# Moved weight loads, a third sample-state buffer, and two chunks of gate rows loaded first in the last stage of a hybrid decoder step

## The chip, the cores and the metric

The kernel runs on one core of one Trainium2 chip. The metric is the device time of one execution in microseconds. The core has four compute engines with a queue each, worked off strictly in order: PE (TensorE, matrix products and transposes), DVE (VectorE), ACT (ScalarE), POOL (GpSimd). SP (SyncE) issues DMAs here, and POOL issues some as well. An instruction that waits for a semaphore holds up everything behind it on its queue.

## The reference, cut to what matters

One step of a one-layer decoder: a joint input projection, then dilated window attention (8 heads of 64) beside an mLSTM (4 heads of 128, chunks of 128), each gated, then one output projection. It does so for a prompt of 2048 tokens and for 8 sample sequences of 4 tokens.

```python
u = rmsnorm(x, norm_g) @ w_in                      # q,k,v,z of attention | q,k,v,o,z,i,f of the mLSTM
# attention, for (window, dilation) in (128,1), (512,4), (2048,16): blocks of 128 queries by 256 keys
s = einsum(qs, kk) * HEAD_DIM_ATT ** -0.5; m = max(s); p = exp(s - m); den = sum(p); acc = einsum(p, vv)
y_a = combine(the three parts) * silu(za)
# mLSTM, chunk by chunk with the state C, n, m
dmat = exp(where(causal, b[t] - b[s] + i[s] - m_t, -inf))
num = inter * (qc @ C) + ((qc @ kc.T) * dmat) @ vc
C = decay * C + (w * kc).T @ vc
y_b = headnorm(sigmoid(ob) * num / den) * silu(zb)
y = rmsnorm(x + concat(y_a, y_b) @ w_out)
# outputs also: the new key/value windows (for the samples: the old cache shifted by 4 rows), and C, n, m
```

## The kernel before, in words

The kernel is written with a tile framework. A scheduler in it fixes at build time the order of the instructions on each engine; memory reuse becomes semaphore waits. `behind_all` and `issue_after` act on that order only. There are three stages.

The first (to about 560 us) makes the projections that attention needs, stores q, k, v to scratch in DRAM, and does the sample tokens' attention.

The second (about 560 to 877 us) is the prompt's attention: four pairs of heads, `pr` 0 to 3, two heads `h` each, 19 batches of at most 512 scores per head. `pair_loads` (L696) brings a pair's `qn` (1 MB) and `kn` (1.5 MB), single buffers. `stacks` (L708) transposes them on PE for one head: 16 blocks of `qn`, 32 of `kn`. A batch is then: scores on PE (L1046, L1047, `ps_s`), mask and minimum on DVE (L1055), shift on POOL (L1057) or ACT, exp on ACT, transposes on PE (L1068, `ps_t`), two halves by ACT and DVE (L1071, L1072), value products on PE (L1084 to L1086, `ps_o`). The values of a pair come in 1 + 4 + 16 loads, v2, v1 and v0 (L978, L981, L984). Into this stage the scheduler weaves the sample tokens' mLSTM, class `SampleMLSTM`: `prepare`, then for each of 8 sequences `state`, which loads a state matrix (L919, 256 KB), multiplies it, stores `dm_num` (L943), adds to it and stores it (L922). Into this stage it also weaves an early part of the last stage's projections (`early`, from `early_x` and the weight blocks `wb`, 2 MB each, loaded at L1117 and L1118 after the first head). `bulk` (L293) starts copies of 1 MB from DRAM to DRAM on POOL's queue, 64 in all, for the samples' new windows; three batches of each head start one (L1063 to L1065).

The last stage (about 877 to 1517 us) goes over 16 chunks of 128 tokens. For each it loads `z` (L1271), the attention parts `A` (L1273, 792 KB), the gate rows `Mb` and, but for chunk 0, `qi` (L1279, L1282; 256 KB each, a DRAM row spread over all partitions), and the residual `xn` (L1286). The mLSTM part adds the causal mask `big` to `Mb` on POOL (L1385), starts three bulk copies there, takes exp on ACT (L1389), multiplies with the scores into `W` on DVE (L1394), and PE makes `ps_num` from `W` (L1406). `merge` (L1424 on) joins the three attention parts. Woven between are the next chunks' projections: `ps_v`, `ps_og`, and `ps_qk` with a convolution on ACT (L1201, L1205), DVE (L1211) and POOL.

"Join" below is the passage from the second stage to the last. The opening of the last stage stands at L1499 to L1509 and the loop at L1518; `A` of chunk 0 needs the three stores of the last pair's attention parts (L1128 to L1130), which go through POOL's queue.

Of the kernel before, what the change touches and what calls it, by code (L numbers as in the profile page):

```python
# [16 lines left out]
ALU = mybir.AluOpType  # L17
# [4 lines left out]
P = 128  # L22
# [815 lines left out]
class SampleMLSTM:  # L838


    def __init__(self, G, I, O, T, pool, pp):
        self.G, self.I, self.O, self.pool, self.pp = G, I, O, pool, pp
        at = 0

        def cut(n, rows=P, back=None):
            nonlocal at
            if back is not None:
                return T[:rows, back:back + n]
            at += n
            return T[:rows, at - n:at]  # L850

        four = lambda x: x.rearrange("p (c b j) -> p c b j", c=8, b=NB)
        heads = lambda x: x.rearrange("p (h e) -> p h e", h=HB)
        self.pre = four(cut(8 * NB * 7))
        self.d, self.th, self.tmp = (four(cut(8 * NS)) for _ in range(3))
        self.cv = four(cut(8 * NB * 3))
        self.kw, self.kz = cut(512, NS, 0), cut(512, NS, 512)
        self.num = heads(cut(HB * 129, NTOK, 1024))
        at = 1024 + HB * 129
        self.qk = cut(8 * NS).rearrange("p (c r) -> p c r", c=8)  # L860
        self.u = cut(1024, NS, at)
        self.C = [heads(cut(HB * 129)) for _ in range(2)]
        self.Dm, self.W = heads(cut(HB * NS, NS)), heads(cut(HB * NS, NS))
        self.qi = heads(cut(HB * NS))
        self.sn = [cut(NS).rearrange("p (b h) -> p b h", h=HB) for _ in range(2)]
        self.bm = cut(NS + NB, NS)
        self.v = heads(cut(HB * 129, NS))

    def ps(self, name):
        return self.pp.tile([P, 512], F32, tag="d", name=name)  # L870
# [13 lines left out]
    def prepare(self):  # L884
# [27 lines left out]
        for h in range(HB):  # L912
            hs = slice(h * P, (h + 1) * P)
            nc.scalar.activation(self.kw[:, hs], pk[:NS, hs], AF.Copy, scale=G.scols[:, 1, h:h + 1])
        self.load(0)

    def load(self, b):
        nc = self.G.nc
        nc.sync.dma_start(out=self.C[b % 2][:, :, 0:128], in_=self.I["state_C"][b].rearrange("h d e -> d h e"))  # L919

    def store(self, b):
        self.G.nc.sync.dma_start(out=self.O["s_C"][b].rearrange("h d e -> d h e"), in_=self.C[b % 2][:, :, 0:128])  # L922

    def state(self, b):
        G, nc, v = self.G, self.G.nc, self.v
        if b:
            self.store(b - 1)
        if b + 1 < NB:
            self.load(b + 1)
        Cb = self.C[b % 2]  # L930
        nc.gpsimd.tensor_copy(Cb[:, :, 128], self.sn[0][:, b])
        rows = slice(b * NTOK, (b + 1) * NTOK)
        nc.gpsimd.tensor_scalar(self.kz, self.kw, self.bm[:, NS + b:NS + b + 1], 0.0, ALU.mult, ALU.add)
        num = self.num
        pn = self.ps("ps_dn")[:, 0:129]
        group = lambda h: pn[h * NS:h * NS + NTOK]
        for h in range(HB):
            nc.tensor.matmul(group(h), lhsT=self.W[:, h, rows], rhs=v[:, h], start=True, stop=False)
        for h in range(HB):
            nc.tensor.matmul(group(h), lhsT=self.qi[:, h, rows], rhs=Cb[:, h], start=False, stop=True)  # L940
        for h in range(HB):
            nc.scalar.activation(num[:, h], group(h), AF.Copy)
        nc.sync.dma_start(out=G.dm_num[rows], in_=num)  # L943
        for a in range(2):
            pc = self.ps("ps_dC")[:, 0:2 * 129].rearrange("p (h e) -> p h e", h=2)
            for j in range(2):
                h = 2 * a + j
                nc.tensor.matmul(pc[:, j], lhsT=self.kz[:, h * P:(h + 1) * P], rhs=v[:, h], start=True, stop=True)
                nc.vector.scalar_tensor_tensor(Cb[:, h], Cb[:, h], G.sdec[:, h * NB + b:h * NB + b + 1], pc[:, j], ALU.mult, ALU.add)
        nc.gpsimd.tensor_copy(self.sn[1][:, b], Cb[:, :, 128])  # L950
# [6 lines left out]
def phase_b(G, I, O, dT):  # L957

    nc, tc = G.nc, G.tc
    with ExitStack() as st:  # L960
# [74 lines left out]
        def head(L, h):  # L1035
# [4 lines left out]
            for nb, batch in enumerate(batches(units(st))):  # L1040
# [18 lines left out]
                        nc.scalar.activation(pr[:, x:x + n], sc[:, x:x + n], AF.Exp, scale=-1.0, bias=nm)  # L1059
                if by_pool:  # L1060
                    nc.scalar.activation(pr[:, :w], sc[:, :w], AF.Exp)
                if nb in (3, 9, 15):
                    beat = pool.tile([P, 1], F32, tag="beat", name="beat")  # L1063
                    bulk(G, 1, nc.gpsimd.tensor_copy(beat, nm))
                with tc.high_priority(offset=60):  # L1065
# [29 lines left out]
        def early():  # L1095
# [4 lines left out]
            for i in range(NO):  # L1100
                G.first.og.append((yield from G.mix.gate_steps(G.early_x, slice(i * P, (i + 1) * P), bank)))

        early = early()
        for pr in range(4):
            L = loads(pr)
            for h in range(2):
                if pr == h == 0:
                    SM.loads()
                n = 2 * pr + h
                if 1 <= n <= 4:  # L1110
                    SM.state(2 * n - 2)
                head(L, h)
                if pr == h == 0:
                    with behind_all(G, last_on(G, ENG.PE, ENG.Activation, ENG.DVE, ENG.Pool)):
                        SM.prepare()
                    for j in range(3):
                        nc.sync.dma_start(out=G.wb[j], in_=G.w_scr[j])  # L1117
                    nc.sync.dma_start(out=G.early_x.rearrange("p a k t -> p (a k t)"), in_=G.x_scr[0])  # L1118
                if 1 <= n <= 4:
                    SM.state(2 * n - 1)  # L1120
                if n == 4:
# [121 lines left out]
def phase_c(G, I, O):  # L1243

    nc, tc = G.nc, G.tc
    with ExitStack() as st:
# [17 lines left out]
            nc.sync.dma_start(out=x16.rearrange("p a k t -> p (a k t)"), in_=G.x_scr[g])  # L1264
            return x16

        def loads(c):
            rows = slice(c * P, (c + 1) * P)
            T = Ctx()
            T.z = pool.tile([P, 2, 512], F32, tag="z", name="z", bufs=2)  # L1270
            nc.sync.dma_start(out=T.z.rearrange("p a c -> p (a c)"), in_=G.z_scr[rows, :])  # L1271
            T.A = pool.tile([P, 3, HA, ROW], F32, tag="wf", name="A", bufs=2)
            nc.sync.dma_start(out=T.A.rearrange("p a (r h) e -> p (a r) (h e)", r=4), in_=G.att_scr.rearrange("a r t e -> t (a r) e")[rows])  # L1273
            return T

        def gate_rows(c, T):
            gr = G.g_scr.rearrange("a (h c) t -> a c h t", h=HB)
# [101 lines left out]
        def mlstm(c, T, qk, tok, v, og, y):  # L1379
            Mb = T.Mb  # L1380
            if c:
                qi = T.qi
                for h in range(HB):
                    nc.gpsimd.tensor_tensor(qi[:, h], qi[:, h], qk[h][:, tok], ALU.mult)  # L1384
            bulk(G, 3, nc.gpsimd.tensor_tensor(Mb, Mb, big.unsqueeze(1).broadcast_to([P, HB, P]), ALU.add))  # L1385
            ps = pp.tile([P, 512], F32, tag="st", name="ps_st", bufs=3)
            pk = pp.tile([P, 512], F32, tag="st", name="ps_kt", bufs=3)
            for h in range(HB):
# [111 lines left out]
        xg = [G.early_x, x_load(1)]  # L1500
        big = one.tile([P, P], F32, tag="big", name="big")
        nc.sync.dma_start(out=big, in_=I["c_causal"])
        L = loads(0)
        gate_rows(0, L)
        for j in range(2):
            nc.sync.dma_start(out=wo[j], in_=G.w_scr[4 + j])
        residual(0, L)
        fg = one.tile([P, D], F32, tag="fg", name="fg")
        nc.sync.dma_start(out=fg, in_=I["final_norm_g"].partition_broadcast(P))  # L1509
        prev = None  # L1510
# [7 lines left out]
        for c in range(NT - 1):  # L1518
# [13 lines left out]
            if c == 3:  # L1532
                run(sample)
            if c + 1 < NT:
                Ln = loads(c + 1)
            if prev is not None:
                next(prev)
                if c < NT - 2:
# [11 lines left out]
                sample = sample_out(ys)  # L1550
                next(sample)
            L = Ln
            gate_rows(c + 1, L)
        gate_rows(NT - 1, Ln)
        spare = G.early_x.rearrange("p a k t -> p (a k t)").bitcast(F32)
        yl = gated(NT - 1, Ln, qk, slice(P, 2 * P), vs[NT - 1], ogs[NT - 1], spare[:, :D])
# [183 lines left out]
```

## Time and profile before

| | us |
|---|---|
| three runs | 1514.84, 1516.72, 1519.55 (median 1516.72) |
| profiled execution, its own time | 1518.98 |
| its span (first to last instruction) | 1517.1 |
| PE busy | 1367.1 (90% of the span) |
| DVE busy | 982.2 (65%) |
| ACT busy | 739.1 (49%) |
| POOL busy | 468.3 (31%) |
| mean busy share of the 16 DMA engines, second stage | 0.5 to 0.9 by slices |

The span leaves out 1.88 us of the profiled execution (1518.98 - 1517.1). PE is busy nearly all of the time, so time can only go where PE stands idle or runs at the lower clock, or by taking work off it. A row of the trace's timeline gives the start, the duration, the engine, line, operation and tiles, and in brackets the idle time before it with what ended it. For an SP row the duration includes the time for which the issue was held up on its queue.

### The profile page before, as it was taken

Reading aid. Unit: us, or ns where it says so; the run is one execution under the profiler, and the core shown is the slowest. Engines: PE = TensorE matmul, PEld = TensorE weight load, DVE = VectorE, ACT = ScalarE, POOL = GpSimd, SP = SyncE. Lnnn points to the kernel's source line nnn. Section 1 sums busy time; section 2 is a strip of 40 time slices with the busy share of each in tenths; the row PEclk is TensorE's granted clock in tenths of the full one; section 3 lists DMA queues with packets and bytes.
Section 4 is the critical chain, followed back from the end, with each engine's and each line's share of the span. In section 5 each row is a group of like instructions: output and inputs, shape, how many; then the busy total and the mean of one; then the engine's idle time right before and its main releaser. Section 6 shows DMA issues by size and latency. Waiting matters only on the chain.

```text
span 1517.1 us, 29006 instructions
## 1 busy us (share of the span) xinstructions
PE 1367.1 (90%) x10679; PEld 851.1 (56%) x10679; DVE 982.2 (65%) x3054; ACT 739.1 (49%) x1701; POOL 468.3 (31%) x797
## 2 busy tenths in 40 slices
PE   4889998989999999579999986789899999999996
PEld 2345444444433348568789854455566666666653
DVE  5663775777643459478888805667766666666665
ACT  5265434454334339578888813344444444444432
POOL 1362334453310016344469922211211111111110
PEclk9999999999999999799999997989999999999999
DMA  8353588768769938884967765752656556643212
GB/s 296 111 181 135 177 284 297 275 218 309 269 216 381 331 128 284 306 264 156 278 216 234 280 218 173 206 174 75 213 161 190 161 188 160 187 161 106 78 48 77
DMA packets 153404, 310.96 MB, mean 205 GB/s; under 512 B 13533, under 2 KB 102782, under 8 KB 142686
## 3 DMA queue, kind: packets, MB, share of 16 engines
q1 hardware_dynamic: 149166, 230.10, 47.9%
q0 software_dynamic: 3952, 78.75, 14.3%
q8 instruction: 84, 1.38, 0.4%
q14 instruction: 58, 0.48, 0.1%
q10 hardware_dynamic: 144, 0.26, 0.0%
HBM read 231.80 MB, written 144.38 MB: 248 GB/s over the span
## 4 chain that ended last, share of the span: by engine, by line
PE 29%; DMA 21%; DVE 14%; issue 6%; ACT 6%; POOL 5%; SPq 2%; POOLq 0%; ACTq 0%; DVEq 0%
DMA Mb<-g_scr 5%; DMA qi<-g_scr 4%; PE ps_t L1068 3%; DVE cd L1211 3%; DMA qn<-q_scr 3%; POOL d_kv L396 2%; PE ps_out L184 2%; PE ps_out L182 2%; PE ps_out L183 2%; DMA v<-v_scr 2%; PE ps_proj L182 2%; PE ps_proj L183 2%; PE ps_proj L184 2%; DMA d_qb<-ds_scr 2%; PE ps_dv L445 2%
## 5 line engine op out<-in xcount | busy, mean ns | idle before, releaser
L182 PE MATMUL ps_proj<-wa,x 128*128 128x512 f16 x640 | 245.7, 386 | 17.9 <-DVE t L541 10.8
L183 PE MATMUL ps_proj<-wa,x 128*128 128x512 f16 x640 | 246.5, 386 | 2.3 <-POOL wa L128 2.0
L184 PE MATMUL ps_proj<-wa,x 128*128 128x512 f16 x640 | 246.5, 385 | 1.0 <-ACT x L243 1.0
L1055 DVE CUSTOM_DVE_ANT_0 sc<-ps_s,mask,ncqk 128x256 f32<-128x256 f32 (+1 forms) x384 | 143.7, 421 | 18.3 <-PE ps_s L1047 15.8
L1057 POOL TENSOR_SCALAR sc<-sc,o 128x256 f32<-128x256 f32 (+1 forms) x272 | 113.9, 430 | 95.7 <-DVE o L1055 90.2
L182 PEld LDWEIGHTS <-x 128*128 128x128 f16 x768 | 73.7, 99 | 100.8 <-issue 16.8
L1072 DVE SCALAR_TENSOR_TENSOR tl<-ps_t,th 128x512 f16<-128x512 f32 (+1 forms) x152 | 103.1, 680 | 38.3 <-ACT th L1071 37.5
L1211 DVE SCALAR_TENSOR_TENSOR cd<-pre,cw,cd 128x256 f32<-128x256 f32 x168 | 88.2, 531 | 53.7 <-ACT cd L1205 52.0
L184 PEld LDWEIGHTS <-x 128*128 128x128 f16 x768 | 73.4, 99 | 85.5 <-issue 12.3
L183 PEld LDWEIGHTS <-x 128*128 128x128 f16 x768 | 73.4, 99 | 77.9 <-issue 9.7
L396 POOL TENSOR_TENSOR d_kv<-d_kv,d_qb 128x512 f32<-128x512 f32 x64 | 85.9, 1376 | 90.7 <-DMA d_qb<-ds_scr 81.2
L1071 ACT ACTIVATE th<-ps_t 128x512 f16<-128x512 f32 (+1 forms) x152 | 90.5, 595 | 41.5 <-PE ps_t L1068 38.9
L184 PE MATMUL ps_out<-wo,yt 128*128 128x512 f16 x256 | 95.6, 382 | 7.8 <-DVE yt L1308 7.0
L1068 PE MATMUL ps_t<-c_id,pr 128*128 128x128 f32 x600 | 98.9, 285 | 2.9 <-DVE tl L1072 2.5
L182 PE MATMUL ps_out<-wo,yt 128*128 128x512 f16 x256 | 98.3, 384 | 3.3 <-ACT pre L1201 2.2
L183 PE MATMUL ps_out<-wo,yt 128*128 128x512 f16 x256 | 98.0, 383 | 0.0
L1385 POOL TENSOR_TENSOR Mb<-Mb,big 128x512 f32<-128x512 f32 x16 | 20.8, 1299 | 249.3 <-DMA Mb<-g_scr 231.7
L1084 PE MATMUL ps_o<-v,th 128*128 128x65 f16 x600 | 78.3, 194 | 13.5 <-DMA dT<-state_C 10.2
L1389 ACT ACTIVATE Mb<-Mb,gcols 128x128 f32<-128x128 f32 x64 | 20.5, 390 | 124.9 <-POOL Mb L1385 124.9
L1384 POOL TENSOR_TENSOR qi<-qi,qk 128x128 f32<-128x128 f32 x60 | 29.2, 515 | 163.7 <-DMA qi<-g_scr 154.4
L1085 PE MATMUL ps_o<-v,th 128*128 128x64 f16 x600 | 77.5, 195 | 0.0
L399 DVE TENSOR_REDUCE d_sc<-d_kv 128x8 f32<-128x512 f32 x64 | 43.1, 677 | 48.1 <-POOL d_kv L396 47.8
(466 smaller groups left out, 3781.6 us busy)
## 6 DMA issues: line engine op xcount, KB each, us to landing
s_win_k<-cache_win_k POOLq DMA_DIRECT2D x32, 1022.0 KB, 8.5
s_win_v<-cache_win_v POOLq DMA_DIRECT2D x32, 1022.0 KB, 8.2
wf<-w_in SPq DMA_DIRECT2D x18, 1024.0 KB
d_kv<-cache_win_k SPq DMA_DIRECT2D x16, 1024.0 KB
d_kv<-cache_win_v SPq DMA_DIRECT2D x16, 1024.0 KB
A<-att_scr SPq DMA_DIRECT2D x16, 792.0 KB
w_scr<-wst SPq DMA_DIRECT2D x12, 1024.0 KB
att_scr<-o SPq DMA_DIRECT2D x9, 1056.0 KB
```

The source lines that it names most:

```text
L182: nc.tensor.matmul(ps, lhsT=xh, rhs=hi[:, kt, cols], start=kt == 0, stop=False)
L183: nc.tensor.matmul(ps, lhsT=xh, rhs=lo[:, kt, cols], start=False, stop=False)
L184: yield nc.tensor.matmul(ps, lhsT=xl, rhs=hi[:, kt, cols], start=False, stop=kt == KT - 1)
L396: nc.gpsimd.tensor_tensor(p, p, qb[:, i], ALU.mult)
L1055: nc.vector.tensor_tensor_reduce(sc[:, x:x + n], sp[:, x:x + n], G.mask[:, MASK_END[u[0]] - n:MASK_END[u[0]]], G.ncqk, BIG, ALU.add, ALU.m ...
L1057: nc.gpsimd.tensor_scalar(sc[:, x:x + n], sc[:, x:x + n], -1.0, nm, ALU.mult, ALU.add)
L1068: nc.tensor.transpose(out=tp[:, c * P:(c + 1) * P], in_=pr[:, c * P:(c + 1) * P], identity=G.idf)
L1071: nc.scalar.activation(th[:, :w], tp[:, :w], AF.Copy, scale=PSC)
L1072: nc.vector.scalar_tensor_tensor(tl[:, :w], tp[:, :w], PSC, th[:, :w], ALU.mult, ALU.subtract)
L1084: nc.tensor.matmul(o, lhsT=th[:, cs], rhs=V[:, 0:65], start=first, stop=False)
L1085: nc.tensor.matmul(o[:, 0:64], lhsT=th[:, cs], rhs=V[:, 66:130], start=False, stop=False)
L1211: eng.scalar_tensor_tensor(d, pre[:, j:j + 256], cw[:, ct, j:j + 1], d, ALU.mult, ALU.add)
```

## The change

Four parts. (1) The weight blocks `wb` 0, 1, 2 were loaded one behind the other after the first head, with `early_x`, ahead of the second pair's `qn` and `kn`. Now block 0 is loaded with the second pair, block 1 at the third head of the eight counted on, block 2 with the third pair, each behind whatever SP holds at that point; `early_x` comes behind the second pair's `kn`. (2) The sample states get three buffers in place of two; the load of state b+2 is issued after the `dm_num` store of b, two are loaded at the start. (3) The last head starts two bulk copies in place of three, and chunk 0 of the last stage none in place of three. Their number stays 64, so the later chunks take them up. (4) The opening loads the gate rows of chunks 0 and 1 right behind `big`, and then `z`, `A`, the residual and the rest.

```diff
         self.C = [heads(cut(HB * 129)) for _ in range(2)]
...
+        self.C.append(heads(cut(HB * 129)))
...
-        self.load(0)
+        for b in range(2):
+            self.load(b)
...
     def state(self, b):
...
-        if b + 1 < NB:
-            self.load(b + 1)
-        Cb = self.C[b % 2]
+        Cb = self.C[b % 3]
...
         nc.sync.dma_start(out=G.dm_num[rows], in_=num)
+        if b + 2 < NB:
+            self.load(b + 2)
...
-                if nb in (3, 9, 15):
+                if nb in ((3, 9) if L.pr == 3 and h else (3, 9, 15)):
                     beat = pool.tile([P, 1], F32, tag="beat", name="beat")
                     bulk(G, 1, nc.gpsimd.tensor_copy(beat, nm))
...
+        def weights(j):
+            with behind_all(G, last_on(G, ENG.SP)):
+                nc.sync.dma_start(out=G.wb[j], in_=G.w_scr[j])
+
         early = early()
         for pr in range(4):
             L = loads(pr)
+            if pr == 1:
+                weights(0)
+                nc.sync.dma_start(out=G.early_x.rearrange("p a k t -> p (a k t)"), in_=G.x_scr[0])
+            elif pr == 2:
+                weights(2)
             for h in range(2):
...
                     SM.state(2 * n - 2)
+                    if n == 2:
+                        weights(1)
                 head(L, h)
                 if pr == h == 0:
...
-                    for j in range(3):
-                        nc.sync.dma_start(out=G.wb[j], in_=G.w_scr[j])
-                    nc.sync.dma_start(out=G.early_x.rearrange("p a k t -> p (a k t)"), in_=G.x_scr[0])
...
-            bulk(G, 3, nc.gpsimd.tensor_tensor(Mb, Mb, big.unsqueeze(1).broadcast_to([P, HB, P]), ALU.add))
+            masked = nc.gpsimd.tensor_tensor(Mb, Mb, big.unsqueeze(1).broadcast_to([P, HB, P]), ALU.add)
+            if c:
+                bulk(G, 3, masked)
...
-        L = loads(0)
-        gate_rows(0, L)
...
-        residual(0, L)
+        L, second = Ctx(), Ctx()
+        gate_rows(0, L)
+        gate_rows(1, second)
+        z_load(0, L)
+        with behind_all(G, last_on(G, ENG.SP)):
+            att_load(0, L)
+        with behind_all(G, last_on(G, ENG.SP)):
+            residual(0, L)
...
-                Ln = loads(c + 1)
+                Ln = loads(c + 1, None if c else second)
...
-            gate_rows(c + 1, L)
+            if c:
+                gate_rows(c + 1, L)
```

The scheduler makes of this other orders on the engines. On SP, in the kernel before, behind the loads of the sample mLSTM's inputs (`dT<-sg_scr` and `dT<-dm_u` are the last of them):

```order
L881 DMA dT_5238<-sg_scr_76 128x128
L882 DMA dT_5238<-dm_u_73 32x4x128
L1117 DMA wb0_5239<-w_scr_69 128x8192
L1117 DMA wb1_5240<-w_scr_69 128x8192
L1117 DMA wb2_5241<-w_scr_69 128x8192
L1118 DMA early_x_5242<-x_scr_67 128x4096
L696 DMA qn_4909<-q_scr_63 128x16x256
L696 DMA kn_4910<-k_scr_64 128x6144
L919 DMA dT_5238<-state_C 128x4x128 x2
```

In the changed kernel, at the same place:

```order
L882 DMA dT_5238<-sg_scr_76 128x128
L883 DMA dT_5238<-dm_u_73 32x4x128
L696 DMA qn_4909<-q_scr_63 128x16x256
L696 DMA kn_4910<-k_scr_64 128x6144
L1114 DMA early_x_5242<-x_scr_67 128x4096
L921 DMA dT_5238<-state_C 128x4x128 x2
L894 DMA s_convT<-dT_5238 128x192
L980 DMA v2_6843<-v_scr_65 128x4160
```

Here `qn_4909` and `kn_4910` are the single buffers of a pair's rows, now of the second pair; three weight blocks and `early_x` no longer stand ahead of them.

On PE, in the kernel before, after a batch of the first pair's second head (`th_6281` are its exponents) the second pair's first transposes (`ps_k_6902`) stand here:

```order
L1084 MATMUL ps_o_6292<-v2_5268,th_6281 128x65
L1085 LDWEIGHTS th_6281
L1085 MATMUL ps_o_6292<-v2_5268,th_6281 128x64
L708 LDWEIGHTS qn_4909
L708 MATMUL ps_k_6902<-idh_85,qn_4909 128x128
L708 LDWEIGHTS qn_4909
```

In the changed kernel the same transposes stand after an earlier batch, whose exponents are `tl_5570`:

```order
L1087 LDWEIGHTS th_5569
L1087 MATMUL ps_o_5580<-v1_5269,th_5569 128x64
L1088 LDWEIGHTS tl_5570
L1088 MATMUL ps_o_5580<-v1_5269,tl_5570 128x65
L708 LDWEIGHTS qn_4909
L708 MATMUL ps_k_6902<-idh_85,qn_4909 128x128
```

In the kernel before, that same product of `tl_5570` is followed by further value products and scores of the first pair:

```order
L1086 MATMUL ps_o_5580<-v1_5269,tl_5570 128x65
L1084 LDWEIGHTS th_5604
L1084 MATMUL ps_o_5580<-v1_5269,th_5604 128x65
L1085 LDWEIGHTS th_5604
L1085 MATMUL ps_o_5580<-v1_5269,th_5604 128x64
L1046 LDWEIGHTS qn_4909
L1046 MATMUL ps_s_5819<-qn_4909 128x256
```

So the transposes of `qn` have moved forward on PE, by 20 batches counted in `ps_t` groups, past all that stands between the two places.

On SP, second pair's small value loads `v0_6848` (16 in all), in the kernel before (`dT` from `state_C` and to `s_C` are sample states):

```order
L696 DMA kn_4910<-k_scr_64 128x6144
L984 DMA v0_6848<-v_scr_65 8x16x260 x2
L1130 DMA att_scr_68<-o0_5292 128x16x132
L922 DMA s_C<-dT_5238 128x4x128
L984 DMA v0_6848<-v_scr_65 8x16x260 x10
L943 DMA dm_num_74<-dT_5238 4x516
L984 DMA v0_6848<-v_scr_65 8x16x260 x4
L922 DMA s_C<-dT_5238 128x4x128
```

In the changed kernel (`v0_6845`):

```order
L696 DMA kn_4910<-k_scr_64 128x6144
L986 DMA v0_6845<-v_scr_65 8x16x260 x2
L1140 DMA att_scr_68<-o0_5292 128x16x132
L986 DMA v0_6845<-v_scr_65 8x16x260 x8
L924 DMA s_C<-dT_5238 128x4x128
L986 DMA v0_6845<-v_scr_65 8x16x260 x3
L943 DMA dm_num_74<-dT_5238 4x516
L986 DMA v0_6845<-v_scr_65 8x16x260 x3
L1107 DMA wb0_5239<-w_scr_69 128x8192
```

The store to `s_C` stood behind two of the sixteen loads and now stands behind ten; weight block 0 follows them.

On SP at the join, in the kernel before (`Mb_11999` is of chunk 0, `Mb_12317` of chunk 1, `Mb_12794` of chunk 2):

```order
L1502 DMA big_11993<-c_causal 128x128
L1271 DMA z_11995<-z_scr_66 128x1024
L1273 DMA A_11997<-att_scr_68 128x12x132
L1279 DMA Mb_11999<-g_scr_78 128x4x128
L1286 DMA xn_12003<-x 128x1024
L1509 DMA fg_12005<-final_norm_g 128x1024
L1271 DMA z_12209<-z_scr_66 128x1024
L1273 DMA A_12211<-att_scr_68 128x12x132
L1286 DMA xn_12213<-x 128x1024
L1279 DMA Mb_12317<-g_scr_78 128x4x128
L1282 DMA qi_12319<-g_scr_78 128x4x128
L1264 DMA early_x_5242<-x_scr_67 128x4096
```

In the changed kernel (`Mb_11994`, `Mb_11996`, `qi_11998` are the gate rows of chunks 0 and 1):

```order
L1521 DMA big_11990<-c_causal 128x128
L1296 DMA Mb_11994<-g_scr_78 128x4x128
L1296 DMA Mb_11996<-g_scr_78 128x4x128
L1299 DMA qi_11998<-g_scr_78 128x4x128
L1286 DMA z_12000<-z_scr_66 128x1024
L1291 DMA A_12002<-att_scr_68 128x12x132
L1303 DMA xn_12004<-x 128x1024
L1533 DMA fg_12006<-final_norm_g 128x1024
L1286 DMA z_12210<-z_scr_66 128x1024
L1291 DMA A_12212<-att_scr_68 128x12x132
L1303 DMA xn_12214<-x 128x1024
```

Both chunks' gate rows stand ahead of `z` and of `A_12002`, behind which they stood before.

## Rows read from the trace of the kernel before

**Rows 1.** Page, busy time of each engine.
```profile
PE 1367.1 (90%) x10679; PEld 851.1 (56%) x10679; DVE 982.2 (65%) x3054; ACT 739.1 (49%) x1701; POOL 468.3 (31%) x797
```
**Rows 2.** Waits from 560 to 920 us: total, times, longest.
```profile
PE ps_k L708 <- DMA qn<-q_scr: 19.1, 2, 16.0
PE ps_o L1084 <- DMA dT<-state_C: 10.2, 1, 10.2
```
**Rows 3.** Timeline of SP at the second pair's loads: start, us.
```profile
592.60 2.58 SPq L1117 DMA_DIRECT2D wb<-w_scr  x3
595.88 0.78 SPq L696 DMA_DIRECT2D qn<-q_scr  x1
596.76 21.66 SPq L696 DMA_DIRECT2D kn<-k_scr  x1
```
**Rows 4.** Timeline of PE, first two heads and after.
```profile
581.46 0.60 PE L1068 MATMUL ps_t<-c_id,pr 128*128 128x128 f32 x4
...
605.90 0.20 PE L1085 MATMUL ps_o<-v,th 128*128 128x64 f16 x1
...
622.14 1.04 PE L708 MATMUL ps_k<-idh,qn 128*128 128x128 f16 x8 [16.05 <-DMA qn<-q_scr]
```
**Rows 5.** Page, DMA issues: KB each, median us to landing.
```profile
s_win_k<-cache_win_k POOLq DMA_DIRECT2D x32, 1022.0 KB, 8.5
...
x_scr<-x POOLq DMA_DIRECT2D x8, 1024.0 KB, 5.6
```
**Rows 6.** Timeline of SP at the second pair's values.
```profile
644.14 0.70 SPq L696 DMA_DIRECT2D qn<-q_scr  x1
657.94 5.21 SPq L922 DMA_DIRECT2D s_C<-dT  x1
663.21 10.15 SPq L984 DMA_DIRECT2D v<-v_scr  x10
673.77 1.78 SPq L984 DMA_DIRECT2D v<-v_scr  x4
```
**Rows 7.** Timeline of PE, third pair's transposes and the wait for values.
```profile
658.30 0.61 PE L708 MATMUL ps_k<-idh,qn 128*128 128x128 f16 x8
...
672.38 0.27 PE L1047 MATMUL ps_s<-kn,qn 128*128 128x256 f16 x1
682.86 0.22 PE L1084 MATMUL ps_o<-v,th 128*128 128x65 f16 x1 [10.21 <-DMA dT<-state_C]
```
**Rows 8.** Timeline of SP at the opening of the last stage.
```profile
872.15 0.33 SPq L1502 DMA_DIRECT2D big<-c_causal  x1
886.43 0.66 SPq L1279 DMA_DIRECT2D Mb<-g_scr  x1
```
**Rows 9.** Chain of waits, 870 to 930 us, in order of time.
```profile
877.82 7.89 DMA att_scr<-o
898.45 21.45 DMA Mb<-g_scr
923.50 0.70 DVE W L1394
```
**Rows 10.** Timeline of POOL at the opening.
```profile
896.50 1.27 POOL L1385 TENSOR_TENSOR Mb<-Mb,big 128x512 f32<-128x512 f32 x1 [15.88 <-DMA Mb<-g_scr]
897.71 1.54 POOL L293 DMA_DIRECT2D s_win_k<-cache_win_k  x3
```
**Rows 11.** Timeline of PE at the opening.
```profile
899.70 0.27 PE L1191 MATMUL ps_qk<-cx,wb 128*128 128x256 f16 x1 [1.99 <-ACT og L1239]
908.01 0.60 PE L1392 MATMUL ps_kt<-c_id,qk 128*128 128x128 f32 x4
924.24 1.23 PE L1406 MATMUL ps_num<-cv,W 128*128 128x129 f32 x4 [15.63 <-DVE W L1394]
```
**Rows 12.** Windows of the join: busy us of each engine, clock, DMA.
```profile
910.00:920.00 10.00, 0.00 (x0) 0.00 (x0) 0.00 (x0) 0.00 (x0) 0.03 (x1) 0.57 0.30 102
920.00:930.00 10.00, 5.76 (x19) 2.85 (x20) 6.43 (x14) 6.49 (x24) 5.13 (x8) 0.58 0.92 371
```

More of the change, by code (lines that the diff above doesn't have):

```diff
@@ L857, in __init__ @@
         self.kw, self.kz = cut(512, NS, 0), cut(512, NS, 512)
-        self.num = heads(cut(HB * 129, NTOK, 1024))
-        at = 1024 + HB * 129
+        self.num = heads(T[64:64 + NTOK, 0:HB * 129])
         self.qk = cut(8 * NS).rearrange("p (c r) -> p c r", c=8)
@@ L862, in __init__ @@
         self.C = [heads(cut(HB * 129)) for _ in range(2)]
-        self.Dm, self.W = heads(cut(HB * NS, NS)), heads(cut(HB * NS, NS))
+        self.W = heads(cut(HB * NS, NS))
         self.qi = heads(cut(HB * NS))
@@ L867, in __init__ @@
         self.v = heads(cut(HB * 129, NS))
+        self.Dm = heads(cut(HB * NS, NS, at))
+        self.C.append(heads(cut(HB * 129)))
     def ps(self, name):
@@ L914, in prepare @@
             nc.scalar.activation(self.kw[:, hs], pk[:NS, hs], AF.Copy, scale=G.scols[:, 1, h:h + 1])
-        self.load(0)
+        for b in range(2):
+            self.load(b)
     def load(self, b):
         nc = self.G.nc
-        nc.sync.dma_start(out=self.C[b % 2][:, :, 0:128], in_=self.I["state_C"][b].rearrange("h d e -> d h e"))
+        nc.sync.dma_start(out=self.C[b % 3][:, :, 0:128], in_=self.I["state_C"][b].rearrange("h d e -> d h e"))
     def store(self, b):
-        self.G.nc.sync.dma_start(out=self.O["s_C"][b].rearrange("h d e -> d h e"), in_=self.C[b % 2][:, :, 0:128])
+        self.G.nc.sync.dma_start(out=self.O["s_C"][b].rearrange("h d e -> d h e"), in_=self.C[b % 3][:, :, 0:128])
     def state(self, b):
@@ L1265, in x_load, with loads, z_load, att_load @@
             return x16
-        def loads(c):
+        def loads(c, T=None):
+            T = T or Ctx()
+            z_load(c, T)
+            att_load(c, T)
+            return T
+        def z_load(c, T):
             rows = slice(c * P, (c + 1) * P)
-            T = Ctx()
             T.z = pool.tile([P, 2, 512], F32, tag="z", name="z", bufs=2)
             nc.sync.dma_start(out=T.z.rearrange("p a c -> p (a c)"), in_=G.z_scr[rows, :])
+        def att_load(c, T):
+            rows = slice(c * P, (c + 1) * P)
             T.A = pool.tile([P, 3, HA, ROW], F32, tag="wf", name="A", bufs=2)
             nc.sync.dma_start(out=T.A.rearrange("p a (r h) e -> p (a r) (h e)", r=4), in_=G.att_scr.rearrange("a r t e -> t (a r) e")[rows])
-            return T
         def gate_rows(c, T):
```

## The prediction

> **What bounds the kernel now.** I read the busy times first: PE works 1367.1 us of a 1517.1 us span [rows 1], so some 150 us are idle, and the other engines have slack. None of the four parts takes work off PE. What they can change is when PE waits for something loaded. So I read next the waits from 560 to 920 us, which is the second stage and the join, and kept those of PE itself that the change touches. Two stand out: 16.0 us in one piece for `qn`, and 10.2 us in one piece before a product of the values [rows 2]. That view names a sample state load as the releaser of the second; the instruction is a value product, and the last value loads are issued at 673.77, nine microseconds before PE resumes at 682.86 [rows 6, 7], so I take those as the true cause. Third is the join: PE stands idle for 15.63 us before `ps_num` of chunk 0 and 1.99 us before that [rows 11]; between 910 and 920 us PE, DVE and ACT do nothing at all [rows 12]. These three, 44 us with the small one, are what the change can reach. Last I read SP's timeline at each of the three places, since it is the queue that the change reorders, and the order of PE before and after.
>
> **The weight blocks.** Before, SP issues three blocks of 2 MB at 592.60 and only then `qn` at 595.88; PE gets it at 622.14, that is 26.3 us after the issue, behind 7 MB [rows 3, 4]. In the changed order `qn` takes the place of the first block, so it is issued at about 592.6: what stands ahead of it on SP is unchanged, and it waits for the completion of older loads alone. Loads and copies of 1 MB land 5.6 to 8.5 us after their issue [rows 5]: `qn` is there at 598.2 to 601.1. If the transposes stood where they did (605.90, [rows 4]), the whole 16.05 us would be gone. But the order on PE moves them 20 batches ahead, behind the batch whose transposes are at 581.46 [rows 4] and whose products end about 582.2. PE then stands from 582.2 to between 598.2 and 601.1, which is 16.0 to 18.9 us, and does afterwards the batches that it did before in the time up to 605.90. Against 16.05 us that is 0 to +2.9; the transposes that are done early are missing later, so nothing is gained by them. The bound below is -3, as part of the idle bits inside those batches may close up while PE waits. I take 0, near the lower landing time, since the queue is empty behind `qn`.
>
> The transposes of the third pair move too, five batches forward from 658.30 [rows 7], about 2 us a batch (152 batches in the 317 us of the stage), to some 648 to 650. Their `qn` is issued at 644.14 [rows 6] and would land, by the same two rows, at 649.7 to 652.6. That is a stall of 0 to 4.5 us; I take +1.5. The blocks themselves, 6 MB, now load behind the second and third pair's values; by the order they are first read in the third pair's second head, so I cost them at nothing: the batches up to there hide them. If that cover is gone, the price is the landing of one block, some 17 us (twice 8.5 us for 2 MB), at a place where PE has batches left to do.
>
> **Three state buffers.** Before, the store of a finished state holds SP for 5.21 us at 657.94, with fourteen of the sixteen value loads behind it; the next ten take until 673.36, the last four are out at 675.55, and PE resumes at 682.86 [rows 6, 7]. After, ten of the loads are ahead of that store. The gain is at most the whole stall, 10.21 us, and at least 0 (if the wait for slots, which made ten loads take 10.15 us, sets the end anyway). I take the 5.21 us by which SP is held, -5.2. The earlier state loads cost nothing on PE, because each is needed two states later.
>
> **Bulk copies.** Four copies are moved to later chunks; the last one leaves long before the end, and in the loop POOL has slack [rows 1]. Price 0, bounds -1 to +1, apart from the join.
>
> **The join.** The chain is read backwards: `ps_num` at 924.24 waits for `W` (923.50), which waits on DVE behind a convolution step, which waits on ACT behind the exp of chunk 1's gate rows, which waits for POOL's addition, which waits for `Mb` of chunk 1, issued at 898.45 and 21.45 us on its way [rows 9, 11]. It is issued that late because SP first waits with `A` of chunk 0 for a store that goes out at 877.82 and takes 7.89 us. Chunk 0's own `Mb` is behind that too: issued 886.43, added at 896.50, 10.07 us later [rows 8 to 10]; the exp behind it holds ACT, which makes the 1.99 us at 899.70 [rows 11]. Now `Mb` of both chunks and `qi` are issued directly behind `big` at 872.15 [rows 8], thus at about 873 to 874, and land by about 884 even at 10.07 us. POOL's additions, 1.27 us each [rows 10], are done by 887, the exps soon after, and nothing of PE's waits for them: `W` waits for `ps_st` and PE alone. PE ends `ps_kt` at 908.61, less 1.99, so 906.6, and goes on with `ps_num`: 924.24 - 906.6 = 17.6 us. Beside it the clock is 0.57 and 0.58 of full in the two windows 910 to 930 [rows 12], the lower of the two levels for most of them, after PE has idled since 908.61. PE's 5.76 busy us in the second of them would be some 3.5 to 4.3 at the full level: I take 1.5 us more. What is late next: the gate rows of chunk 2, whose buffer is free only after `W` of chunk 0, hence issued about 905, and POOL's three copies, which no longer start with chunk 0's addition at 897.71 but with chunk 1's, at about 886, when `A`, the residual and `fg` are issued. I take +1.5 for these, bounds 0 to +12 (below). Join: -17.6 - 1.5 + 1.5 = -17.6, between -19.1 and -7.
>
> **Sum.** 0 + 1.5 - 5.2 + 0 - 17.6 = -21.3 us. The profiled execution took 1518.98 us, 1.88 more than its span, and would go to 1497.7. It stands 2.26 us above the median of the runs, 1516.72; from that the forecast is 1495.4, say 1495. The likeliest case's own range is 1485 to 1504.
>
> **Rivals.** First, the stall for `qn` goes as well, 16 us more: 1479. For it: without the three blocks ahead, `qn` lands before the old place of its transposes, 605.90. Against it: the order on PE, and an issue at 592.6 that nothing moves ahead. Only if PE reached the transposes far later than I read would it hold.
>
> Second, the join gives back half. Chunk 1's `Mb` took 21.45 us with three copies just ahead (897.71) and four loads of SP in flight, chunk 0's took 10.07 without them [rows 8 to 10]. If chunk 2's gate rows take 21.45 instead of about 10, they land 11.4 us later, at about 927 in place of 916, and POOL, ACT and then PE wait for them: 1495 + 11 = 1506. The Trainium skill ("DMA: Bandwidth & Descriptors", section "Issuing engines are not separate DMA queues") says that DMAs of all issuing engines end on the same sixteen DMA engines and interleave there; by that, copies on POOL's queue do slow SP's loads, and moving them from chunk 0 to chunk 1 puts them beside the loads of `A` and the residual. The 21.45 us beside the 10.07 us are in line with it.
>
> Third, no difference. `qn` stays as slow as it was: 26.3 us after an issue at 592.6 is 618.9, so PE idles 36.7 in place of 16.05 us, +20.7, which eats the -21.3: 1516. What speaks for it is that the value loads and sample inputs ahead of `qn` are many small pieces; against it, that in the trace 7 MB stood ahead of it and here nothing of that size.
>
> Fourth, slower: the same place and mechanism, transposes that stand ahead of ready batches in an in-order queue, with `qn` later still. It decides from a landing past about 624 us (598.2 + 21.3 and the 5 us of the bound, 0.3%): at 630, PE idles 47.8 us, +31.7, and the time is 1527. Twenty batches that are ready then wait behind one load, where before they covered it.
>
> **Chances.** Forecast 0.57, first rival 0.08, second 0.20, third 0.08, fourth 0.07. About 0.3%, 4.6 us, is what a measurement of this kernel can tell from no change. Faster is the forecast with the first two rivals, 0.85; same 0.08; slower 0.07. The range leaves out the third and fourth and the far half of the first: 1478 to 1509.
>
> **What would show it.** PE's long wait for `qn` at 582 to 599 in place of 606 to 622, of about the same length: that is the step I hold to be least obvious. If the wait is gone or twice as long, that step is wrong. PE's wait for values near 672 to 683 about half as long. At the join, `Mb` of both chunks issued before 875, POOL's two additions before 890, no PE idle time over 2 us between `ps_kt` and `ps_num`, and `ps_num` 17 us earlier relative to the last attention batch. A new PE wait of over 5 us between `ps_num` of chunk 0 and that of chunk 2 would show the second rival; a time over 1512 would mean that the forecast is wrong as a whole.

## The result and the profile after

The changed kernel takes 1496.82 us in the median of four runs (1494.56 to 1502.37); the kernel before takes 1518.13 us in four (1514.84 to 1520.16). The medians differ by 21.3 us; the ratio is 0.9871, with a 95% interval of 0.984 to 0.9902. The forecast was 1495, that is 21.3 us below the median it started from. The profiled execution took 1498.03 us, 20.95 less than that of before.

The sum was right; several of its terms were not. At the places of the long waits, the changed kernel's timeline of PE now has these rows (start, duration, line and tiles, idle time before and its releaser):

```profile
591.86 1.03 PE L708 MATMUL ps_k<-idh,qn 128*128 128x128 f16 x8 [16.25 <-DMA qn<-q_scr]
...
650.14 1.04 PE L708 MATMUL ps_k<-idh,qn 128*128 128x128 f16 x8 [5.15 <-DMA qn<-q_scr]
...
730.88 1.04 PE L708 MATMUL ps_k<-idh,qn 128*128 128x128 f16 x8 [4.54 <-DMA qn<-q_scr]
...
889.22 0.27 PE L1201 MATMUL ps_qk<-cx,wb 128*128 128x256 f16 x1 [0.88 <-ACT og L1249]
...
897.96 0.61 PE L1425 MATMUL ps_num<-cv,W 128*128 128x129 f32 x4
...
921.06 0.37 PE L1201 MATMUL ps_qk<-cx,wb 128*128 128x256 f16 x1 [10.80 <-ACT cv L1240]
```

Read against the rows of before: the wait for `qn` of the second pair is as long as it was (16.25 us against 16.05, [rows 4]) and 30 us earlier. The wait for the values (10.21 us, [rows 7]) is gone. The third pair's transposes, which did not wait [rows 7], wait 5.15 us. At the opening, 1.99 us are now 0.88, the 15.63 us before `ps_num` [rows 11] are gone, and a wait of 10.80 us stands before the second chunk's `ps_qk`.

SP's timeline of the changed kernel shows why the first of these kept its size:

```profile
585.42 0.78 SPq L696 DMA_DIRECT2D qn<-q_scr  x1
586.30 2.03 SPq L696 DMA_DIRECT2D kn<-k_scr  x1
588.42 0.38 SPq L1114 DMA_DIRECT2D early_x<-x_scr  x1
...
637.17 2.76 SPq L696 DMA_DIRECT2D qn<-q_scr  x1
652.92 8.29 SPq L986 DMA_DIRECT2D v<-v_scr  x8
661.51 0.40 SPq L924 DMA_DIRECT2D s_C<-dT  x1
661.95 5.41 SPq L986 DMA_DIRECT2D v<-v_scr  x3
667.77 1.04 SPq L986 DMA_DIRECT2D v<-v_scr  x3
```

`qn` goes out at 585.42 and PE has it at 591.86, 6.4 us later, where before it took 26.3 [rows 3, 4]. The transposes, however, now stand where PE is at 575.6. The last rows are the second pair's value loads: eight go out in one run before the store of a state, and the last at 667.77 against 673.77 [rows 6].

At the opening, SP and POOL of the changed kernel:

```profile
867.93 0.33 SPq L1521 DMA_DIRECT2D big<-c_causal  x1
868.32 0.97 SPq L1296 DMA_DIRECT2D Mb<-g_scr  x2
893.52 0.36 SPq L1291 DMA_DIRECT2D A<-att_scr  x1
893.99 5.94 SPq L1303 DMA_DIRECT2D xn<-x  x1
906.89 0.73 SPq L1296 DMA_DIRECT2D Mb<-g_scr  x1
```
```profile
871.01 1.23 POOL L1140 DMA_DIRECT2D att_scr<-o  x1
886.01 1.27 POOL L1402 TENSOR_TENSOR Mb<-Mb,big 128x512 f32<-128x512 f32 x1 [7.18 <-DMA Mb<-g_scr]
917.87 1.26 POOL L1402 TENSOR_TENSOR Mb<-Mb,big 128x512 f32<-128x512 f32 x1 [27.43 <-DMA Mb<-g_scr]
```

The gate rows of chunks 0 and 1 are issued at 868.3 (before: 886.43 and 898.45, [rows 8, 9]). But the last store of attention parts, issued at 871.01, lets `A` of chunk 0 go only at 893.52: 22.5 us, where it took 7.9 [rows 9]. Everything behind `A` on SP is late by some of that, and the gate rows of chunk 2 go out at 906.89, 11 us after `W` of chunk 0 freed their buffer. They land at 917.87, and POOL, ACT (exp, then `cv`) and PE wait in turn.

### The profile page after: what moved, and what is told of

It reads as the page before. It is cut to its first block, busy times and chain, and to the rows that moved or that the text cites. A ratio compares the mean times of both kernels' runs of the same rounds, so it can differ in the third digit from the quotient of the medians.

```text
span 1496.2 us, 28998 instructions
## 1 busy us (share of the span) xinstructions
PE 1363.8 (91%) x10679; PEld 848.4 (57%) x10679; DVE 979.5 (65%) x3054; ACT 739.1 (49%) x1701; POOL 465.8 (31%) x796
## 4 chain that ended last, share of the span: by engine, by line
PE 29%; DMA 22%; DVE 16%; issue 6%; ACT 5%; POOL 4%; SPq 1%; POOLq 0%; ACTq 0%; DVEq 0%
DMA qi<-g_scr 5%; DMA Mb<-g_scr 5%; PE ps_out L184 3%; DVE cd L1221 3%; PE ps_t L1070 3%; PE ps_out L183 2%; PE ps_out L182 2%; DMA qn<-q_scr 2%; PE ps_proj L182 2%; PE ps_proj L183 2%; DMA z_scr<-z 2%; PE ps_proj L184 2%; POOL d_kv L396 2%; PE ps_dv L445 2%; DVE sc L1057 2%
## 5 line engine op out<-in xcount | busy, mean ns | idle before, releaser
L1221 DVE SCALAR_TENSOR_TENSOR cd<-pre,cw,cd 128x256 f32<-128x256 f32 x168 | 84.5, 508 | 29.4 <-ACT cd L1215 27.6
L1201 PE MATMUL ps_qk<-cx,wb 128*128 128x256 f16 x256 | 71.3, 278 | 11.7 <-ACT cv L1240 10.8
```

Source lines behind the costliest of these rows:

```text
L1221: eng.scalar_tensor_tensor(d, pre[:, j:j + 256], cw[:, ct, j:j + 1], d, ALU.mult, ALU.add)
```

## The experiments

Two profiles of either kernel, one of each variant, and start times of the same instruction counted from the start of its engine's list (the n-th `tl` on DVE is the n-th batch of the attention stage, the n-th `W` the n-th chunk), carry the comparisons. Times in us from the span's start; end is the span; the variants are described below:

| | 1st tl | 25th tl | 51st tl | 121st tl | 9th W | end |
|---|---|---|---|---|---|---|
| before | 568.5 | 624.8 | 687.6 | 824.6 | 1248.5 | 1517.1 |
| before, second profile | 563.0 | 623.0 | 684.8 | 823.8 | 1246.5 | 1514.8 |
| changed | 562.6 | 621.1 | 674.5 | 816.6 | 1227.6 | 1496.2 |
| changed, second profile | 564.1 | 621.0 | 675.2 | 817.7 | 1229.6 | 1502.9 |
| opening alone | 566.1 | 622.8 | 686.8 | 826.3 | 1240.0 | 1509.4 |
| all but the opening | 564.8 | 622.1 | 675.1 | 818.5 | 1241.9 | 1508.4 |
| weights alone | 564.3 | 621.1 | 673.6 | 827.2 | 1255.5 | 1525.3 |
| third buffer alone | 567.4 | 625.2 | 684.6 | 825.4 | 1242.4 | 1511.0 |
| transposes at old place | 564.8 | 610.7 | 668.3 | 811.5 | 1223.8 | 1493.2 |
| gate rows ahead of `big` | 563.3 | 623.9 | 678.1 | 818.1 | 1219.7 | 1489.7 |
| copies as before | 564.8 | 620.4 | 670.1 | 811.6 | 1220.0 | 1488.7 |
| both repairs | 564.4 | 609.6 | 667.9 | 815.3 | 1217.3 | 1486.7 |

From the last batches to the ninth chunk the kernel before takes 423.9 and 422.7 us, the changed one 411.1 and 411.9: the join gives about 11.8 us. Up to the 121st batch the changed kernel is 7.0 us ahead on the average of two: the attention stage gives the rest. How far one profile can be trusted there shows in the five that have the changed kernel's order up to that batch (both of its own, all but the opening, gate rows ahead of `big`, copies as before): they reach it between 811.6 and 818.5, a scatter of 6.9 us; three with the old order reach it between 823.8 and 826.3. At the 51st batch, behind the place of the values, the changed kernel is 11.4 us ahead. What takes some 4.4 us of that back by the 121st is open: the third pair's new wait lies ahead of the 51st batch, and the fourth pair's (4.54 and 2.63 us) is about as long as before (3.09 and 3.49).

**The opening alone.** The kernel before with only the opening's part of the change:

```diff
-        L = loads(0)
-        gate_rows(0, L)
...
+        gate_rows(0, L)
+        gate_rows(1, second)
+        z_load(0, L)
...
+            if c:
+                bulk(G, 3, masked)
```

> The kernel before with the opening alone changed (gate rows of chunks 0 and 1 first, no copies in chunk 0, one copy less in the last head). Theory: the join by itself gives what the two profiles differ by between the last attention batches and chunk 2, 12 to 13 us, so about 1505; the waits of 16 us for qn and of 10 us for the values stay. Rival: the opening only gains because the loads of the weight blocks and states went out of its way; then it gives under 5 us, 1513 or more.

Measured: 1506.65 us (7 runs), ratio to before 0.9926 (0.9899 to 0.9953), 11 us less. By the table the join, from the 121st batch to the ninth chunk, is 9.6 us shorter than the mean of the two profiles of before. A new wait of 11.71 us stands before the second chunk's `ps_qk` here too. The theory holds, and the opening's gain does not depend on the other parts.

**All but the opening.** The reverse edit: the changed kernel with its opening and its copies as before.

> The changed kernel with its opening and its copies put back as before. Theory: the attention stage gives about 2 us net (10 us for the values gone, 5 to 8 us of new waits for qn of the third and fourth pair), so about 1515 to 1516; the 5.9 us by which the first stage was shorter in the profile of the changed kernel are scatter from one execution to the next. Rival: those 5.9 us belong to the change and come back here: about 1509.

Measured: 1508.75 us (10 runs), ratio 0.9936 (0.9911 to 0.9961), 8.8 less. The rival's number came, but not for its reason: the first stage, 5.9 us shorter in the first pair of profiles, was as short in the second profile of the kernel before (563.0). It is scatter, and the waits behind it take it up again (the two profiles of before are 5.5 us apart at the first batch and 0.8 at the 121st). What comes is the attention stage, and my 2 us for it were read from one profile pair with that scatter in it. At the place of the values a wait of 3.73 us stands in this run: smaller than before, but not gone.

**Weights alone, third buffer alone.** The first is the move of the blocks without the third buffer; the second (which also moves two small tiles, `num` and `Dm`, to make room):

```diff
+        self.C.append(heads(cut(HB * 129)))
...
-        if b + 1 < NB:
-            self.load(b + 1)
...
+        if b + 2 < NB:
+            self.load(b + 2)
```

> The kernel before with the weight blocks and early_x moved alone (two state buffers, old opening, copies as before). Theory: the ten-microsecond wait for the values goes by the weights' move alone, since in this order too the first store of a state stands behind ten of the sixteen value loads; the wait for qn stays at about 16 us at its new, earlier place; time within 3 us of the run with everything but the opening (1508.75), so 1506 to 1512. Rival: it is the third buffer that frees the values; then the 10 us wait stays here and the time is 1515 or more.

> The kernel before with the third state buffer alone. Theory: the first store of a state still stands behind only two of the value loads on SP, so the wait for the values stays at 8 to 10 us, the wait for qn at 16 us, and the time is that of the kernel before, 1515 to 1520. Rival: the earlier loads of states free the values: wait under 3 us, time 1508 or less.

Measured: weights alone 1524.6 us (10 runs), ratio 1.0045 (1.0023 to 1.0067), 6 us slower than before; third buffer alone 1509.4 us (6 runs), 0.9938 (0.9911 to 0.9965), 9 us faster. Both theories fell on the time. The first was right about the values: with the weights alone that wait is gone. The wait for `qn` is 11.59 us, not 16. But the states are late now. PE's timeline with weights alone, and SP's there:

```profile
682.39 0.40 PE L940 MATMUL ps_dn<-dT 128*4 128x129 f32 x8 [4.14 <-POOL dT L931]
...
756.29 0.61 PE L940 MATMUL ps_dn<-dT 128*4 128x129 f32 x8 [4.98 <-POOL dT L931]
```
```profile
733.54 15.17 SPq L984 DMA_DIRECT2D v<-v_scr  x12
749.01 0.39 SPq L919 DMA_DIRECT2D dT<-state_C  x1
```

PE waits for POOL's copy into the state tile, which waits for a state's load; the second of these loads stands on SP behind twelve value loads and goes out at 749.01. With two buffers a load can be issued only when the state before it but one has been stored; with three it is ready a state earlier. From the 51st to the 121st batch the weights alone take 153.6 us, all but the opening, which has the third buffer as well, 143.4, and the kernel before 137.0 and 138.9. From 700 to 760 us PE is busy for 47.72 us with the weights alone and for 56.23 before:

```profile
700.00:760.00 60.00, 47.72 (x652) 40.23 (x649) 41.39 (x159) 43.00 (x94) 23.55 (x60) 0.93 0.97 284
```
```profile
700.00:760.00 60.00, 56.23 (x789) 47.84 (x787) 51.24 (x194) 50.53 (x112) 28.35 (x72) 0.97 0.84 259
```

The third buffer alone left the wait for `qn` (16.41 us) and half of that for the values (5.37). Its profile is 2 us ahead of the first one of before at the third `W` and 6 at the ninth; the schedule of the opening came out different in it (PE makes `ps_num` of chunk 0 at 907.1 and waits 11.28 us after it). Up to the 121st batch it is not ahead at all (825.4); its join takes 417.0 us in place of 423. The profiled execution was the slowest of the six, so how the 9 us divide stays open.

By medians, then, the third buffer alone (1509.4 us) is as good as all but the opening (1508.75): the moved weight blocks gain nothing on top of it that the times show. The traces put the two gains at different places, though, the one in the attention stage, the other in the join, and no run separates them further.

**The transposes at their old place.**

```diff
-            if L.pr or h:
-                stacks(G, h, st, lambda: ppk.tile([P, 1024], F16, tag="pk", name="ps_k"))
+            with behind_all(G, [G.anchor[L.pr]] if h == 0 and L.pr in G.anchor else []):
+                if L.pr or h:
+                    stacks(G, h, st, lambda: ppk.tile([P, 1024], F16, tag="pk", name="ps_k"))
...
+                if h and nb == {1: 2}.get(L.pr + 1):
+                    G.anchor[L.pr + 1] = last_on(G, ENG.PE)[0]
```

> The changed kernel with the second pair's first transposes held at the place on PE that they had before (20 batches later). Theory: what is left of the weight blocks' move is hidden by that order; qn is there before PE comes to it, the wait of 16.2 us goes, and the time falls by 14 to 18 us from the changed kernel, to about 1481. Rival: the work behind the transposes is what counts, and the wait only turns into waits of DVE and ACT at the start of the second pair: 1492 to 1497.

Measured: 1495.11 us (4 runs), 0.9851 of before (0.9814 to 0.9888), within 2 us of the changed kernel. The wait for `qn` is gone as foreseen, and so is most of its worth: the rival's time came. The transposes now start without idle time before them:

```profile
603.78 0.61 PE L708 MATMUL ps_k<-idh,qn 128*128 128x128 f16 x8
```

The windows show where the worth went. First the changed kernel, then this one:

```profile
580.00:600.00 20.00, 8.14 (x84) 7.45 (x85) 4.26 (x15) 4.16 (x8) 2.48 (x6) 0.57 0.80 259
600.00:620.00 20.00, 19.95 (x321) 18.86 (x320) 19.76 (x84) 19.87 (x44) 12.85 (x33) 1.00 0.32 103
```
```profile
580.00:600.00 20.00, 17.20 (x247) 15.44 (x244) 17.14 (x76) 15.22 (x37) 10.55 (x28) 0.91 0.70 233
600.00:620.00 20.00, 15.91 (x226) 14.94 (x224) 13.78 (x48) 14.94 (x30) 12.05 (x26) 0.91 0.85 292
```

In the changed kernel PE, DVE and ACT rest for most of 580 to 600 and then run without a pause, DVE at 19.76 of 20 us: the transposes and their evictions, done early, are out of the way. Here the batches go on during 580 to 600, and the second window has the transposes among them, with DVE at 13.78 us. So the lead over the changed kernel is spent step by step: 10.4 us at the 25th batch, 6.2 at the 51st, 5.0 at the 121st, 3.8 at the ninth chunk. The last three are no more than the scatter above: copies as before, with the changed kernel's order and a wait of 13.16 us for `qn`, is 4.9 us ahead at the 121st batch too. What is shown is that most of the 16 us is not gained; whether 2 or 5 us are, these runs can't tell.

**Gate rows ahead of `big`.**

```diff
+        gate_rows(0, L)
+        gate_rows(1, second)
         big = one.tile([P, P], F32, tag="big", name="big")
...
-        gate_rows(0, L)
-        gate_rows(1, second)
         z_load(0, L)
```

> The changed kernel with the gate rows of chunks 0 and 1 issued ahead of big, which waits on SP until about 868 us. Theory: the slow landing of the gate rows delays the last store of attention parts, and so A of chunk 0, and so all that SP issues behind it, the gate rows of chunk 2 among them; issued some 10 us earlier they leave the store alone, A of chunk 0 goes out before 886, the 10.8 us of PE at 921 shrink to under 4, and the time falls by 6 to 10 us from the changed kernel, to about 1488. Rival: the three copies that start with chunk 1 make the gate rows of chunk 2 late; then the wait stays at about 10 us and the time at 1497.

Measured: 1492.24 us (4 runs), 0.9829 of before (0.979 to 0.9867), 4.6 less than the changed kernel. SP's timeline of this kernel, POOL's last store of attention parts, and PE at the place of the 10.80 us:

```profile
858.71 0.92 SPq L1296 DMA_DIRECT2D Mb<-g_scr  x2
869.49 0.35 SPq L1524 DMA_DIRECT2D big<-c_causal  x1
883.22 0.37 SPq L1291 DMA_DIRECT2D A<-att_scr  x1
899.44 0.75 SPq L1296 DMA_DIRECT2D Mb<-g_scr  x1
```
```profile
872.57 1.23 POOL L1140 DMA_DIRECT2D att_scr<-o  x1
```
```profile
915.03 0.27 PE L1201 MATMUL ps_qk<-cx,wb 128*128 128x256 f16 x1 [1.63 <-ACT og L1249]
```

The gate rows go out at 858.71, `A` of chunk 0 at 883.22 (893.52 in the changed kernel), the gate rows of chunk 2 at 899.44 (906.89), and the wait is 1.63 us (10.80). The store takes 10.7 us (22.5). The theory holds in each step, and the join, from the 121st batch to the ninth chunk, is 401.6 us, some 10 us less than the changed kernel's. Of the 6 to 10 us foreseen for the whole time only 4.6 came in the medians, with ranges that overlap (1488.86 to 1496.19, 1494.56 to 1502.37).

The store's time goes with the place of the gate rows in all twelve profiles. From its issue to that of `A` it is 21.4 to 24.6 us in the five with the gate rows of two chunks issued at most 5.3 us ahead of it, 6.6 to 8.2 in the five with the old opening, and 10.7 and 12.1 in the two with the gate rows 13.9 us ahead.

**Copies as before.** The changed kernel with the three copies of chunk 0 and the last head's third one put back (the edit of `bulk` and of `nb` undone).

> The changed kernel with the bulk copies as before (three in chunk 0, three in the last head). Theory: the gate rows of chunks 0 and 1 are loaded before any of these copies starts, so the copies of chunk 0 touch only the last store, A and the residual; the wait of 10.8 us of PE at 921 grows by 0 to 5 us; 1496 to 1502. Rival: leaving out the copies was what made the opening quick; then PE waits 15 us or more before chunk 1 or 2 and the time is 1505 or more.

Measured: 1497.54 us (4 runs, 1490.43 to 1500.56), 0.9847 of before (0.9811 to 0.9883): no difference from the changed kernel. The long wait of PE at the opening is 8.94 us here and stands one step later, but it has the same cause. The gate rows of chunk 2, issued at 905.51, hold ACT before its exp, and what PE waits for stands behind that on ACT:

```profile
920.30 1.28 ACT L1406 ACTIVATE Mb<-Mb,gcols 128x128 f32<-128x128 f32 x4 [8.10 <-POOL Mb L1402]
```
```profile
925.14 1.03 PE L1323 MATMUL ps_yt<-idh,yh 128*128 128x128 f16 x8 [8.94 <-ACT yh L1362]
```

The copies neither made nor cost the gain: the store takes 21.4 us with them and 22.5 without, and the join 408.4 us beside 411.1 and 411.9.

**Both repairs.** Gate rows ahead of `big`, and the transposes anchored at batch 0 in place of 2. Counted by the batches' `tl` on DVE, 9 batches stand ahead of these transposes in the changed kernel, 24 in the kernel before and 22 here. So the change had moved them by 15 batches, not by the 20 that were counted ahead of the result, and this anchor is not halfway but two batches before the old place.

> The changed kernel with the gate rows ahead of big, and the second pair's first transposes held back to a place on PE halfway between the old and the new one. Theory: both repairs add up: no wait for qn over 4 us in the second pair, no wait of PE over 3 us at the opening; the gate rows give 5 us as measured, the transposes 2 to 7, so 1485 to 1491. Rival: what the transposes gain is taken back in the attention stage by DVE and ACT, which work at their limit behind the wait: 1491 to 1494.

Measured: 1486.73 us (4 runs, 1483.07 to 1488.43), 0.9775 of before (0.9742 to 0.9807): 10 us below the changed kernel and the fastest of all, as the theory had it. PE has no wait over 6 us between 560 and 1000 us; the largest are 5.13 and 5.07, neither of them for `qn`, and the opening has none over 2 us. Beside the gate rows alone (1492.24) the transposes are worth 5.5 us here, beside the changed kernel 1.7 in the run with the old place; the runs behind each of these medians spread over 5 to 8 us, so the two worths do not contradict each other.

**Either kernel again.**

> The kernel before, unchanged, profiled a second time. If the first stage's 5.9 us between the two profiles are scatter, its end (first batch's tl on DVE, 568.48 in the first profile) is here anywhere from 562 to 568; if it belongs to where the weight blocks stand, it is again at 566 to 569. The three long waits (16 us qn, 10 us values, 16 us ps_num) come back within 2 us.

> The changed kernel, unchanged, profiled a second time. If the first stage is scatter its end is anywhere from 562 to 568, else again at 562 to 565. The wait of 16 us for qn comes back within 2 us; the wait of 10.8 us at the opening, if it is made by the order of the loads and not by chance, comes back at 8 to 13 us, with A of chunk 0 issued over 20 us after its last store.

Measured: 1516.7 and 1504.65 us, one run each. The long waits came back: 15.45, 8.64 and 15.77 us in the kernel before, 13.46 and 10.64 in the changed one, with `A` of chunk 0 issued 23.6 us after its last store. The 13.46 is 2.8 us below the first profile's 16.25, more than the 2 us foreseen. The first stage ends at 562.95 and 564.11, so it is scatter.

## Why the prediction was right, and where it was not

*The weight blocks.* The mechanism was right. `qn` came 6.4 us after its issue (5.6 to 8.5 foreseen), and the place of the wait was the one that the order on PE gave, though the transposes had moved by 15 batches and not by 20. PE waited 16.25 and 13.46 us in the two profiles, 13.2 to 16.6 in the three others with this order; 16.0 to 18.9 was foreseen, so the wait is at the lower end or below it. The first rival, that the stall goes, failed because of that order. And 16 us of waiting turned out to be worth little: by medians 1.7 us in the run with the old place, 5.5 in the one with both repairs. Behind the wait PE, DVE and ACT are busy for over 19.7 of 20 us each, and which of them sets the pace there no run separates. The term for the third pair was too small: 5.15 and 4.78 us, above my bound of 4.5. The step that failed is the landing: 5.6 to 8.5 us were taken from copies elsewhere, and this `qn` took 13.0 us from its issue at 637.17. (Its transposes had moved by three batches, not five; PE reached them at 645.0.)

*The values.* Mis-sized: -5.2 was taken; in the changed kernel the whole 10.21 us went (in all but the opening, 3.73 stayed). And the prediction put it under the third buffer, which was half wrong. It is the weights' move that brings ten loads ahead of the store and removes the wait (the third buffer alone halves it, to 5.37 us); but by itself that costs 6 us, as the loads of the states fall behind. The third buffer is what makes the move harmless. Up to the 121st batch the two terms and the third pair's come to 7.0 us; the prediction had 5.2 - 1.5 = 3.7. Of the 7.0 the waits explain 10.2 - 5.2 = 5.0; the rest is within the scatter.

*The join.* The chain was right: gate rows first, no wait before `ps_num` (it is at 897.96, without idle time before it), and the wait for `og` down to 0.88. The give-back of +1.5 was mis-sized: 10.8 and 10.6 us of new wait. The second rival had the place, the gate rows of chunk 2, and its price, 11 us. It had the time as well, if it is counted from the 121st batch, since the whole stage came 8 us earlier: the rival's landing at 927 is 102.4 us behind that batch, the forecast's at 916 is 91.4, and 101.3 and 101.9 were measured. Its cause was another: not slow rows beside the copies, which make no difference, but SP's queue. The rows took 11 us, as in the forecast, and went out 10 us late. Three loads of gate rows are on their way while the last store is, the store takes 22.5 us, `A` waits for it, and all behind `A` waits. The Trainium skill ("DMA: Bandwidth & Descriptors", section "Issuing engines are not separate DMA queues") has DMAs of all issuing engines interleave on the same DMA engines. The store, on POOL's queue, agrees with it: 22.5 us beside SP's gate rows, 10.7 when they had gone ahead. For the copies against the gate rows, the use that the prediction made of it, no run shows an effect. I had costed that step (`A` behind the store) as unchanged at 7.9 us: this is the step of the prediction that failed.

The net of the join is 11.8 us, not 17.6. With 10.8 in place of 1.5 the prediction's own terms would give 8.3; the rest comes from later waits, which shrank, and from the clock. From the 121st batch to the third chunk PE's idle time fell from 30.7 and 32.3 us to 21.3 and 22.2, and its busy time by about 2.6 us for the same work, where the prediction had 1.5 for the clock (0.58 of its 5.76 us would be 3.3, not 3.5 to 4.3, so its own rows gave up to 2.4). The granted clock did come up, from 0.91 and 0.92 in that stretch to 0.96 and 0.95: 0.76 and 0.73 in the windows that had 0.57 and 0.58 [rows 12]. It was not full there, and PE still rests at 910; in the run with the gate rows ahead of `big`, where PE is busy for 8.37 us from 910 to 920, it is 1.00 in that window.

The changed kernel's windows:

```profile
910.00:920.00 10.00, 0.26 (x2) 0.00 (x0) 0.59 (x4) 0.84 (x3) 2.13 (x3) 0.76 0.53 155
920.00:930.00 10.00, 8.94 (x63) 7.13 (x63) 6.76 (x15) 4.85 (x14) 3.07 (x4) 0.73 0.91 316
```

So -3.7 became about -7, and -17.6 about -11.8; the errors have opposite signs. The mechanisms were mostly right, but that the total of 21.3 us agrees with the forecast to a tenth is luck: its terms do not deserve it. By medians the parts add up: opening -10.9, the rest -8.8, together -19.6 against -21.3.

## What to carry to other kernels

A load that is moved forward is worth what the in-order queue of its reader lets it be: look where the reader moved, too. Before you credit a removed wait, see which engines have no slack right behind it. Before you price a stage from one pair of profiles, see how far two profiles of one kernel differ there. And when loads are put ahead of a store on which the queue then waits, cost the store's landing anew, not from the trace of before.

## What the runs showed of the hardware that was not expected

Gate rows, 256 KB each and one DRAM row spread over all partitions, are slow for their size. In the changed kernel those of chunk 1, beside chunk 0's, a `qi` and the store, took 17.15 us (chain of waits), though the DMA engines were busy only a third of 870 to 880 (windows):

```profile
868.80 17.15 DMA Mb<-g_scr
```
```profile
870.00:880.00 10.00, 10.00 (x48) 4.58 (x47) 0.00 (x0) 1.22 (x4) 3.90 (x4) 1.00 0.34 95
880.00:890.00 10.00, 9.12 (x61) 5.78 (x60) 0.00 (x0) 4.50 (x13) 3.97 (x8) 1.00 0.70 216
```

So it is not the mean load of the DMA engines that a late transfer of this kind is to be judged by. Why these loads are slow was not tried.
